# The entry of the two FFNs of a hybrid encoder step: wider vector instructions, another order of operand preparation, and two lent weight tiles

## The chip, the cores and the metric

One core of one Trainium2 chip runs the whole program. The metric is the device time in microseconds of one execution, the median of some runs. TensorE (PE) multiplies matrices; VectorE (DVE), ScalarE (ACT) and GpSimd (POOL) work element by element; SyncE (SP) issues most transfers (DMA). Each engine works through its own instructions in order and waits on semaphores for the others.

## The reference

A two-layer encoder step on 1088 columns (1024 prompt frames and 64 sample frames) of width 1024, all in fp32. Each layer has a mixer (SSD in layer 0, attention in layer 1) and then the SwiGLU FFN, each between two norms:

```
x = x + rmsnorm(mixer(rmsnorm(x, n0)), n1)
x = x + rmsnorm(swiglu(rmsnorm(x, n2), w_in, w_out), n3)
swiglu(u) = (silu(u @ w_gate) * (u @ w_up)) @ w_out
```

The hidden width is 2816, that is 22 slices of 128. The change touches the way from the mixer's projection to the first slices of `swiglu` in both layers, and the weight loads of the rest of the FFN.

## The kernel before, in words

fp32 products are built from reduced-precision ones: every operand is split in a high part (a cast on ACT, "cast") and a low part (operand minus high part, a subtraction on DVE, "low"), and three matmuls h·xh, h·xl, l·xh take the place of one. So each weight tile and each activation tile needs a cast and a low before PE can use it; the first matmul of a product needs both high parts, the second the activation's low, the third the weight's low.

PE's order is written by hand: a planner (`Stream`) spawns side tasks after given delays in modelled PE time (`CHW` holds such delays for the norms). The order on the other engines comes from a scheduler with priorities: code under `tc.high_priority(k)` is issued ahead of lower ones. Once issued the order on an engine is fixed.

The FFN of a layer (`back`) runs so. The columns are in four quarters `QS` of 256, 256, 288 and 288. `start` projects a quarter (`mmx` matmuls); `chain` then applies the post-norm (L1178), adds x (L1179, which arrives by DMA in `xr`, L1169 and L1175), squares (ACT, L449 and L452), sums the squares over eight tiles (POOL, L453), lets PE add over partitions (`nst`, L461), forms the reciprocal root, spreads it (`nbp` on PE, `rb` on ACT, L492) and applies the pre-norm (L1190). Quarters 0 and 1 make block 0 (n = 256 per half), quarters 2 and 3 block 1 (n = 288).

`op_build` makes a block's operands for Strassen-like products: a11, a12, a21, a22 (two halves of the channels by two quarters) and the sums s3, s2, s1, s4 (L1107, L1140). Each is split (cast L1119, low L1120).

First `plain_pairs` runs five slices of block 0 by ordinary products (`mmx`, L427 to L429) on a11 to a22 alone. Then `run_pair` runs double pairs: seven products P1 (weight r0, operand a11), P6 (ta, s2), P2 (r0, a12), P7 (ta, s3), P5 (tb, s1), P4 (tb, a22), P3 (b22, s4) per block, twelve matmuls each, into `px` tiles in PSUM (four of them), whose results DVE and ACT take out (L1257 to L1277). Here r0, b22 are weights, ta and tb sums of them (L262, L263 on POOL, L280, L281 on DVE). In the first double pair, t = 5, block 0's seven products run ahead of block 1's seven (`apart`); afterwards the blocks alternate. At the end stand five single-block pairs and then the product with `w_out` (`po`).

Weights go through a raw ring of two tiles (L224, 512 KB each), then cast L312 and low L313 into a ring `hl` of three. A raw tile is free when its last reader is done, an `hl` slot when PE has read it.

Of the kernel before, what the change touches and what calls it, by code (L numbers as in the profile page):

```python
# [1 line left out]

# [10 lines left out]
ALU = mybir.AluOpType  # L13
# [25 lines left out]

GAP_A, GAP_B = 1.8, 1.2  # L40
RB_WAIT = 4.8
CHW = ((13.1, 8.8, 18.0), (7.5, 6.0, 20.5)), ((9.0, 5.2, 18.0), (10.5, 8.0, 21.0))
AT_W1, AT_W2 = 6.0, 2.5
SSD_GAP, SSD_D = 4.4, 6.5
ST_W, ST_RB = (6.5, 22.0, 22.0), (6.0, 1.0, 1.0)
# [152 lines left out]
            c["ring"][1] += 1  # L198


class Weights:


# [2 lines left out]
    def __init__(self, nc, raw, hl, half, tt):  # L206
        self.nc, self.raw, self.hl, self.half, self.tt = nc, raw, hl, half, tt

        self.tc, self.pri = None, 0
        self.lq, self.sq, self.ready, self.eng = [], [], [], None  # L210

        self.hx, self.used = Ring(None, "hx", 0, hl.shape, hl.dtype), []

    def plan(self, *items):
        for it in items:
            it = dict(it)
            it["raw"] = []
            self.lq.append(it)
            self.sq.append(it)

    def load(self):
        it = self.lq[0]
        r = self.raw.get()
        self.nc.sync.dma_start(r[:, :it.get("n", 1024)], it["src"][len(it["raw"])])  # L224
        it["raw"].append(r)
        if len(it["raw"]) == len(it["src"]):
            self.lq.pop(0)

    def advance(self):
        moved = True  # L230
        while moved:
            moved = False
            while self.lq and self.raw.free():
# [8 lines left out]
    def plain(self, it):  # L242
        if not self.room():
            return False
        r, n = it["raw"][0], it.get("n", 1024)
        if it.get("kscale") is not None:
            self.scaled(it, r)
        else:
            self.part(it, "w", None, r[:, :n])
        self.raw.put()  # L250
        self.ready.append(self.sq.pop(0))
        return True

    def pair(self, it):
        r0, r1 = it["raw"]
        b11, b21, b12, b22 = r0[:, :512], r0[:, 512:], r1[:, :512], r1[:, 512:]
        if "T" not in it:
            if not self.tt.free(2):
                return False
            ta, tb = it["T"] = self.tt.get(), self.tt.get()  # L260
            g = self.nc.gpsimd.tensor_tensor
            g(ta[:, 512:], b22, b12, op=ALU.subtract)  # L262
            g(tb[:, :512], b12, b11, op=ALU.subtract)  # L263
            return True
        ta, tb = it["T"]
        if "b22" not in it and self.half.free():
            self.part(it, "b22", self.half, b22, self.nc.gpsimd)
            self.raw.put()
            return True
        if "r0" not in it:  # L270
            if not self.hl.free():
                return False
            self.part(it, "r0", self.hl, r0)
            self.ready.append(it)

            return False
        if "sums" not in it:
            v = self.nc.vector.tensor_tensor
            with self.tc.high_priority(self.pri):
                v(ta[:, :512], ta[:, 512:], b11, op=ALU.add)  # L280
                v(tb[:, 512:], b21, ta[:, :512], op=ALU.subtract)  # L281
            self.raw.put()
# [64 lines left out]
def hybrid_kernel(  # L347
# [48 lines left out]
    W.tc = tc  # L396
    UC = Cells(384, (R, 99))
    DG = Ring(nsb, "dg", DGB, [P, 3, P])

# [687 lines left out]
    def op_build(ops, done, when=lambda: True):  # L1087
# [14 lines left out]
        def total(nm_, x_, y_, op, eng):  # L1102
            yield 0, 0, R.free if nm_ == "s3" else some
            t, rg[nm_] = take(R) if nm_ == "s3" else take(*rings)
            L[nm_] = v4(t, n)
            with tc.high_priority(OPP[ops.layer][ops.b]):
                eng.tensor_tensor(L[nm_], L[x_], L[y_], op=op)  # L1107
            yield 0, OS[ops.b]

# [22 lines left out]
            ("s1", "a21", "a22", ALU.add, V), ("s4", "a12", "s2", ALU.subtract, V),  # L1132
        )
        if ops.b:
            for x in sums:
                if x[0] not in L:
                    yield from total(*x)
                else:
                    with tc.high_priority(OPP[ops.layer][ops.b]):
# [12 lines left out]
        rg["a12"].put()  # L1152
        for nm_ in ("a21", "a22", "s2", "s1", "s4", "s3"):
            yield from split(nm_)

    def chain(layer, q, y, ss, cw, xsrc, xout, cpre, done):
# [1 line left out]
        o, n = QS[q]  # L1158

        rings = (RX, R) if q < 2 else (R,)  # L1160

        def some():
            return any(r.free() for r in rings)

        w_post, w_rb, w_pre = CHW[layer][q // 2]
        yield 0, w_post, some
        t, r = take(*rings)
        xr = v4(t, n)
        nc.sync.dma_start(xr, xsrc[:, 0:4, o:o + n])  # L1169
        out = []  # L1170
        yield from rb_steps(ss, n, out, w_rb)
        s2 = ssum_start(n)
        for m in range(KD):
            if m == 4:
                nc.sync.dma_start(xr, xsrc[:, 4:8, o:o + n])  # L1175
            ym = y[m // 4][:, m % 4, :]
            with tc.high_priority(CHP[layer][q // 2]):
                V.scalar_tensor_tensor(ym, ym, col(cw + m), out[0], op0=ALU.mult, op1=ALU.mult)  # L1178
                (V if m % 2 else G).tensor_tensor(ym, ym, xr[:, m % 4, :], op=ALU.add)  # L1179
                add_sq(s2, ym, n, m == 0)  # L1180
            if m % 4 == 3:
# [104 lines left out]
    def back(layer, start, cpost, xsrc, xmid, cpre, cpost2, xout, rb_out, done2):  # L1286
# [3 lines left out]
        with ExitStack() as es:  # L1290
# [103 lines left out]
            with ExitStack() as e2:  # L1394
# [27 lines left out]
            phase[0] = 2  # L1422

            W.pri = LDP
            xss, more = {}, None
# [538 lines left out]
```

## Time and profile before

| | us |
|---|---|
| median of 3 runs | 3045.68 (3041.55 to 3046.09) |
| the profiled execution | 3046.85 |
| its span in the trace | 3045.2 |
| PE busy | 2981.5 |
| DVE busy | 2075.4 |
| ACT busy | 1463.6 |
| POOL busy | 816.2 |

Mean granted clock of PE: 0.993. The times of the rows below count from the start of the span. A row of waits says which instruction of an engine waited, for whose result, how long in all and how often. A row of a timeline shows one instruction or a run of like ones; instructions that follow each other directly overlap by some 0.08 us, so the starts tell the spacing. In a row of windows the clock 1.00 is 2.4 GHz and 0.50 is 1.2 GHz.

### The profile page before, as it was taken

To read this page: it belongs to the slowest core of one execution; us is meant where nothing else is said; L and a number is where in the kernel's file an instruction comes from. 1 tells how busy PE (TensorE), PEld (TensorE's weight loads), DVE (VectorE), ACT (ScalarE), POOL (GpSimd) and SP (SyncE) were. 2 spreads that over 40 slices of the span, in tenths; PEclk is the share of its full clock that TensorE was granted. 3 is DMA by queue.
4 is the path that set the end of the run, shared out by engine and by line. 5 is a ranking of instruction groups with operands and counts; after the bars stand their busy time and mean duration, and the time that the engine had idled before them with its cause. 6 is when DMAs were issued, how large, how long until landed. Compare 5 with 4: busy or idle time off the path is not lost. (4 is left out here: it accounts for less than half of the span.)

```text
span 3045.2 us, 56936 instructions
## 1 busy us (share of the span) xinstructions
PE 2981.5 (98%) x21785; PEld 2913.9 (96%) x21785; DVE 2075.4 (68%) x4498; ACT 1463.6 (48%) x2703; POOL 816.2 (27%) x975
## 2 busy tenths in 40 slices
PE   8999999999999999999999999999999999999999
PEld 7899999999999999999999899999999999999998
DVE  7878877786778545584656787777677645575544
ACT  6656666564453222244445665556553322344433
POOL 1323333330434334351222000000154434342111
PEclk9999999999999999999999999999999999999999
DMA  3011111125554222245655222223455222245654
GB/s 120 33 57 51 58 49 50 60 69 154 170 156 129 81 79 77 80 138 177 205 179 158 86 85 72 63 65 100 129 154 154 75 82 78 73 124 179 205 187 139
DMA packets 180097, 333.35 MB, mean 109 GB/s; under 512 B 18128, under 2 KB 128336, under 8 KB 179824
## 3 DMA queue, kind: packets, MB, share of 16 engines
q1 hardware_dynamic: 178032, 323.35, 34.5%
q0 software_dynamic: 1792, 6.36, 1.1%
q8 instruction: 171, 2.80, 0.4%
q14 instruction: 102, 0.84, 0.1%
HBM read 262.59 MB, written 62.60 MB: 107 GB/s over the span
## 5 line engine op out<-in xcount | busy, mean ns | idle before, releaser
L427 PE MATMUL mm<-r,hl 128*128 128x384 f32 (+2 forms) x1664 | 554.7, 333 | 8.4 <-DVE craw L713 4.5
L429 PE MATMUL mm<-r,hl 128*128 128x384 f32 (+2 forms) x1664 | 539.3, 324 | 1.1 <-DVE hl L313 0.6
L428 PE MATMUL mm<-r,hl 128*128 128x384 f32 (+2 forms) x1664 | 538.8, 324 | 0.0
L313 DVE TENSOR_TENSOR hl<-raw,hl 128x1024 fp32r<-128x1024 f32 (+1 forms) x269 | 332.0, 1235 | 299.7 <-ACT hl L312 298.6
L312 ACT CAST hl<-raw 128x1024 fp32r<-128x1024 f32 (+1 forms) x269 | 270.7, 1010 | 263.8 <-DMA raw<-in_w_f_dram 98.8
L1246 PE MATMUL px<-r,hl 128*128 128x288 f32 (+1 forms) x1192 | 349.9, 294 | 0.0
L427 PEld LDWEIGHTS mm<-r,hl 128*128 128x128 f32 x1664 | 315.5, 190 | 11.5 <-issue 5.1
L1245 PE MATMUL px<-r,hl 128*128 128x288 f32 x1056 | 311.5, 295 | 6.1 <-DVE u L1260 6.1
L429 PEld LDWEIGHTS mm<-r,hl 128*128 128x128 f32 x1664 | 314.9, 189 | 2.1 <-DVE hl L325 1.1
L453 POOL TENSOR_TENSOR ssum<-ssum,sq 128x256 f32<-128x256 f32 (+3 forms) x153 | 166.2, 1093 | 559.4 <-ACT sq L452 556.2
L428 PEld LDWEIGHTS mm<-r,hl 128*128 128x128 f32 x1664 | 315.7, 190 | 0.5 <-issue 0.2
L1247 PE MATMUL px<-r,hl 128*128 128x288 f32 x1056 | 310.7, 294 | 0.0
L1247 PE MATMUL px<-rx,hl 128*128 128x256 f32 x816 | 229.3, 281 | 6.7 <-DVE hl L313 6.7
L1245 PE MATMUL px<-rx,hl 128*128 128x256 f32 x816 | 229.8, 282 | 0.0
L1246 PEld LDWEIGHTS px<-r,hl 128*128 128x128 f32 x1192 | 223.9, 188 | 0.1
L1442 PE MATMUL po<-rx,hl 128*128 128x384 f32 (+1 forms) x640 | 206.9, 323 | 0.0
L1245 PEld LDWEIGHTS px<-r,hl 128*128 128x128 f32 x1056 | 198.4, 188 | 8.0 <-DVE u L1260 8.0
L1441 PE MATMUL po<-rx,hl 128*128 128x384 f32 (+1 forms) x608 | 198.5, 326 | 0.0
L1247 PEld LDWEIGHTS px<-r,hl 128*128 128x128 f32 x1056 | 198.2, 188 | 0.0
L1443 PE MATMUL po<-rx,hl 128*128 128x384 f32 (+1 forms) x608 | 197.0, 324 | 0.4 <-DVE hl L313 0.3
L1246 PE MATMUL px<-rx,hl 128*128 128x256 f32 x680 | 190.8, 281 | 0.0
L262 POOL TENSOR_TENSOR tt<-raw 128x512 f32<-128x512 f32 x44 | 60.0, 1364 | 402.7 <-DMA raw<-in_w_f_dram 274.5
(359 smaller groups left out, 8141.5 us busy)
## 6 DMA issues: line engine op xcount, KB each, us to landing
raw<-in_w_f_dram SPq DMA_DIRECT2D x204, 512.0 KB, 3.8
raw<-in_w_in_dram SPq DMA_DIRECT2D x40, 512.0 KB, 3.7
raw<-in_w_f_dram SPq DMA_DIRECT2D x48, 384.0 KB, 3.2
sg<-hscr SPq DMA_DIRECT2D x88, 192.0 KB, 3.6
raw<-in_w_so_dram SPq DMA_DIRECT2D x32, 512.0 KB, 3.9
raw<-in_w_kv_dram SPq DMA_DIRECT2D x18, 512.0 KB, 3.6
raw<-in_w_o_dram SPq DMA_DIRECT2D x16, 512.0 KB, 3.7
sg<-hscr SPq DMA_DIRECT2D x44, 160.0 KB, 3.7
```

The costliest lines, as they stand in the source:

```text
L312: self.nc.scalar.copy(h, v)
L313: (eng or self.eng or self.nc.vector).tensor_tensor(lo, v, h, op=ALU.subtract)
L427: PE.matmul(ps[:, :n], h_, xh, start=(first and i == 0), stop=False)
L428: PE.matmul(ps[:, :n], h_, xl, start=False, stop=False)
L429: PE.matmul(ps[:, :n], l_, xh, start=False, stop=(last and i == nk - 1))
L453: (eng or G).tensor_tensor(ssum[:, :n], ssum[:, :n], q[:, :n], op=ALU.add)
L1245: PE.matmul(ps, wh, ah[:, k, :], start=(k == 0), stop=False)
L1246: PE.matmul(ps, wh, al[:, k, :], start=False, stop=False)
L1247: PE.matmul(ps, wl, ah[:, k, :], start=False, stop=(k == 3))
L1441: PE.matmul(ps[:, :n], wh, xh, start=(k == 0), stop=False)
L1442: PE.matmul(ps[:, :n], wh, xl, start=False, stop=False)
L1443: PE.matmul(ps[:, :n], wl, xh, start=False, stop=(k == FT - 1))
```

## The change

Four parts. (1) `chain` takes two `xr` tiles and loads all of x's quarter at its start; the add and the square run on four tiles at once (add on DVE alone), and the sum of the squares is three DVE additions of 1024, 512 and 256 columns; POOL is no longer in it. In layer 1 the second norm of quarters 0 and 1 is planned after 13 instead of 18 us. (2) `op_build` of block 0 splits a11, a12, a21, a22 ahead of all sums. (3) `op_build` of block 1 waits for `W.lead`, the low part of `ta` of the first double pair, and its sums are issued after it. (4) From the last double pair on, up to two operand tiles `RX` serve as further raw weight tiles, one in the `w_out` stage, none at its very end.

```diff
+class Lent:
+    def __init__(self, ring):
+        self.ring, self.cap, self.live = ring, 0, 0
+    def free(self):
+        return self.live < self.cap and self.ring.free()
...
-CHW = ((13.1, 8.8, 18.0), (7.5, 6.0, 20.5)), ((9.0, 5.2, 18.0), (10.5, 8.0, 21.0))
+CHW = ((13.1, 8.8, 18.0), (7.5, 6.0, 20.5)), ((9.0, 5.2, 13.0), (10.5, 8.0, 21.0))
...
+        if key == "ta" and self.lead is None:
+            self.lead = ins
...
-            with tc.high_priority(OPP[ops.layer][ops.b]):
+            with tc.high_priority(OPP[ops.layer][ops.b]), (tc.issue_after(W.lead.ins) if ops.b else nullcontext()):
                 eng.tensor_tensor(L[nm_], L[x_], L[y_], op=op)
...
         if ops.b:
+            yield 0, 0, lambda: W.lead is not None
             for x in sums:
...
-        for nm_ in ("a11", "a12"):
+        for nm_ in ("a11", "a12", "a21", "a22"):
             yield from split(nm_, True)
         for x in sums:
             yield from total(*x)
...
-        for nm_ in ("a21", "a22", "s2", "s1", "s4", "s3"):
+        for nm_ in ("s2", "s1", "s4", "s3"):
             yield from split(nm_)
...
-        for m in range(KD):
-            if m == 4:
-                nc.sync.dma_start(xr, xsrc[:, 4:8, o:o + n])
-            ym = y[m // 4][:, m % 4, :]
-            with tc.high_priority(CHP[layer][q // 2]):
-                V.scalar_tensor_tensor(ym, ym, col(cw + m), out[0], op0=ALU.mult, op1=ALU.mult)
-                (V if m % 2 else G).tensor_tensor(ym, ym, xr[:, m % 4, :], op=ALU.add)
-                add_sq(s2, ym, n, m == 0)
...
+        with tc.high_priority(CHP[layer][q // 2]):
+            for h in range(2):
+                for m in range(4):
+                    ym = y[h][:, m, :]
+                    V.scalar_tensor_tensor(ym, ym, col(cw + 4 * h + m), out[0], op0=ALU.mult, op1=ALU.mult)
+                V.tensor_tensor(y[h], y[h], xr[h], op=ALU.add)
+                A.activation(xr[h], y[h], AF.Square)
+                nc.sync.dma_start(xout[:, 4 * h:4 * h + 4, o:o + n], y[h])
+            V.tensor_tensor(xr[0], xr[0], xr[1], op=ALU.add)
+            V.tensor_tensor(xr[0][:, 0:2, :], xr[0][:, 0:2, :], xr[0][:, 2:4, :], op=ALU.add)
+            V.tensor_tensor(s2[:, :n], xr[0][:, 0, :], xr[0][:, 1, :], op=ALU.add)
...
                     if t_ == FT - 1:
                         phase[0] = 1
+                        W.lent.cap = 2
                         st.spawn(loader())
```

What this does to the order on DVE, at three places. First, layer 1, where block 0's operands are made. Before, L1190 is the pre-norm of quarter 1, L1107 the sums, L1120 the lows (the row 3040 is that of a21):

```order
3035 L1120 TENSOR_TENSOR rx<-rx 128x1024 x2
3036 L1190 SCALAR_TENSOR_TENSOR rx<-rx,pcs,rb 128x256 x8
3037 L1107 TENSOR_TENSOR r<-rx 128x1024
3038 L1107 TENSOR_TENSOR rx<-rx,r 128x1024
3039 L1107 TENSOR_TENSOR rx<-rx 128x1024 x2
3040 L1120 TENSOR_TENSOR r<-rx,r 128x1024
3041 L1120 TENSOR_TENSOR rx<-rx 128x1024
```

In the changed kernel the same lines are L1218 (pre-norm), L1132 (sums) and L1145 (lows):

```order
3050 L1145 TENSOR_TENSOR rx<-rx 128x1024
3051 L1218 SCALAR_TENSOR_TENSOR rx<-rx,pcs,rb 128x256 x8
3052 L1145 TENSOR_TENSOR rx<-rx 128x1024
3053 L1145 TENSOR_TENSOR r<-rx,r 128x1024
3054 L1145 TENSOR_TENSOR rx<-rx 128x1024
3055 L1132 TENSOR_TENSOR r<-rx 128x1024
3056 L1132 TENSOR_TENSOR rx<-rx,r 128x1024
3057 L1132 TENSOR_TENSOR rx<-rx 128x1024 x2
```

All four lows of a11 to a22 now stand ahead of the sums.

Second, layer 0, the first double pair. Before, L1107 and L1140 are block 1's sums, the first two L313 the lows of ta and tb, L1260 to L1266 take products of block 0 out of PSUM, and the first L1120 is the low of block 1's a11:

```order
1269 L1107 TENSOR_TENSOR r<-r 128x1152 x2
1270 L1140 TENSOR_TENSOR r<-r 128x1152
1271 L313 TENSOR_TENSOR hl<-tt,hl 128x1024
1272 L1221 TENSOR_TENSOR x<-mmx,x 128x256
1273 L1107 TENSOR_TENSOR r<-r 128x1152
1274 L313 TENSOR_TENSOR hl<-tt,hl 128x1024
1275 L1260 TENSOR_TENSOR u_11425<-px,p_11410 128x256
1276 L280 TENSOR_TENSOR tt<-tt,raw 128x512
1277 L1120 TENSOR_TENSOR r<-r 128x1152
1278 L1262 TENSOR_TENSOR p_11410<-px,p_11410 128x256
1279 L1266 TENSOR_TENSOR u_11463<-px,u_11425 128x256
1280 L281 TENSOR_TENSOR tt<-raw,tt 128x512
```

In the changed kernel L335 is the low of ta and then of tb, L302 and L303 are weight sums of the next pair, L1132 and L1167 block 1's sums, L1288 to L1300 the evictions of block 0's products:

```order
1285 L335 TENSOR_TENSOR hl<-tt,hl 128x1024
1286 L1132 TENSOR_TENSOR r<-r 128x1152
1287 L1249 TENSOR_TENSOR x<-mmx,x 128x256
1288 L335 TENSOR_TENSOR hl<-tt,hl 128x1024
1289 L302 TENSOR_TENSOR tt<-tt,raw 128x512
1290 L1288 TENSOR_TENSOR u_11330<-px,p_11315 128x256
1291 L303 TENSOR_TENSOR tt<-raw,tt 128x512
1292 L1132 TENSOR_TENSOR r<-r 128x1152
1293 L1290 TENSOR_TENSOR p_11315<-px,p_11315 128x256
1294 L1167 TENSOR_TENSOR r<-r 128x1152
1295 L1294 TENSOR_TENSOR u_11363<-px,u_11330 128x256
1296 L1132 TENSOR_TENSOR r<-r 128x1152
```

and, right behind these, the evictions of P5 and P4 and the low of block 1's a11 (L1145):

```order
1297 L1297 TENSOR_TENSOR c_11378<-px,u_11363 128x256
1298 L1298 TENSOR_TENSOR u_11330<-px,u_11330 128x256
1299 L1300 TENSOR_TENSOR u_11363<-px,u_11363 128x256
1300 L1145 TENSOR_TENSOR r<-r 128x1152
```

The sums moved from ahead of the low of ta to behind it, in between the evictions; the low of a11 moved behind the eviction of P4, the sixth of block 0's seven products.

Third, the end of the same pair, block 1's products. Before, the last of the seven lows (L1120) is that of s4; the three L313 are the lows of r0, ta and tb of the next pair:

```order
1289 L1120 TENSOR_TENSOR r<-r 128x1152
1290 L1262 TENSOR_TENSOR p_11535<-px,p_11535 128x288
1291 L1120 TENSOR_TENSOR r<-r 128x1152
1292 L313 TENSOR_TENSOR hl<-raw,hl 128x1024
1293 L1266 TENSOR_TENSOR u_11591<-px,u_11554 128x288
1294 L313 TENSOR_TENSOR hl<-tt,hl 128x1024
1295 L1269 TENSOR_TENSOR c_11613<-px,u_11591 128x288
1296 L1270 TENSOR_TENSOR u_11554<-px,u_11554 128x288
1297 L1272 TENSOR_TENSOR u_11591<-px,u_11591 128x288
1298 L313 TENSOR_TENSOR hl<-tt,hl 128x1024
1299 L1277 TENSOR_TENSOR u_11554<-px,u_11554 128x288
```

In the changed kernel the three L335 are these lows, L1300 is the eviction of block 1's P4, and the last L1145 is the low of s4:

```order
1307 L335 TENSOR_TENSOR hl<-raw,hl 128x1024
1308 L1294 TENSOR_TENSOR u_11495<-px,u_11454 128x288
1309 L335 TENSOR_TENSOR hl<-tt,hl 128x1024
1310 L1297 TENSOR_TENSOR c_11521<-px,u_11495 128x288
1311 L1298 TENSOR_TENSOR u_11454<-px,u_11454 128x288
1312 L1300 TENSOR_TENSOR u_11495<-px,u_11495 128x288
1313 L335 TENSOR_TENSOR hl<-tt,hl 128x1024
1314 L1145 TENSOR_TENSOR r<-r 128x1152
```

The low of s4 moved from ahead of all three weight lows to behind them and behind the eviction of P4. Layer 1's first pair has the same order at its end, rows 3157 to 3164.

## Rows read from the trace of the kernel before

**Rows 1.** The page: busy time by engine, and one of its groups.

```profile
PE 2981.5 (98%) x21785; PEld 2913.9 (96%) x21785; DVE 2075.4 (68%) x4498; ACT 1463.6 (48%) x2703; POOL 816.2 (27%) x975
...
L1245 PE MATMUL px<-r,hl 128*128 128x288 f32 x1056 | 311.5, 295 | 6.1 <-DVE u L1260 6.1
```

**Rows 2.** Waits of PE, 2240 to 2372 us: us in total, times, longest.

```profile
PE px L1247 <- DVE hl L313: 3.0, 1, 3.0
PE mmx L428 <- DVE r L1120: 2.5, 1, 2.5
PE mmx L427 <- ACT hl L312: 1.8, 1, 1.8
PE mmx L429 <- DVE hl L313: 0.8, 1, 0.8
```

**Rows 3.** Timeline of PE: start, us, operation, in brackets the idle time ahead and releaser.

```profile
961.54 0.58 PE L1247 MATMUL px<-rx,hl 128*128 128x256 f32 x1 [3.71 <-DVE hl L313]
...
2257.03 0.83 PE L461 MATMUL nst<-ones,ssum 128*128 128x1 f32 x4 [3.59 <-POOL ssum L453]
```

**Rows 4.** Windows: us, busy of PE, PEld, DVE, ACT, POOL, clock, DMA, GB/s.

```profile
972.28:983.45 11.17, 11.17 (x86) 11.17 (x85) 11.17 (x13) 7.26 (x9) 3.08 (x2) 1.00 0.11 30
2281.18:2287.97 6.79, 6.79 (x32) 6.79 (x33) 5.82 (x16) 3.46 (x5) 0.02 (x1) 0.50 1.05 249
2322.11:2328.93 6.82, 6.82 (x34) 6.82 (x33) 4.29 (x15) 0.00 (x0) 0.00 (x0) 0.50 0.66 216
2345.22:2371.28 26.06, 22.94 (x170) 22.44 (x169) 25.15 (x28) 13.73 (x17) 8.82 (x5) 0.93 0.25 79
2349.94:2352.83 2.89, 2.89 (x13) 2.89 (x14) 2.89 (x3) 2.89 (x5) 2.41 (x2) 0.50 0.14 45
```

**Rows 5.** Timeline of DVE, first pair of layer 0: start, us, line, operation.

```profile
967.97 1.35 DVE L1120 TENSOR_TENSOR r<-r 128x1152 fp32r<-128x1152 f32 x1
...
969.57 0.41 DVE L1266 TENSOR_TENSOR u<-px,u 128x256 f32<-128x256 f32 x1
969.90 0.67 DVE L281 TENSOR_TENSOR tt<-raw,tt 128x512 f32<-128x512 f32 x1
...
974.37 3.37 DVE L1120 TENSOR_TENSOR r<-r 128x1152 fp32r<-128x1152 f32 x2
```

**Rows 6.** Timeline of ACT, same stretch; in brackets idle before, and releaser.

```profile
960.34 0.62 ACT L312 CAST half<-raw 128x512 fp32r<-128x512 f32 x1 [5.53 <-DMA raw<-in_w_f_dram]
960.86 1.04 ACT L312 CAST hl<-tt 128x1024 fp32r<-128x1024 f32 x1
```

**Rows 7.** Timeline of POOL, same stretch.

```profile
962.61 2.42 POOL L262 TENSOR_TENSOR tt<-raw 128x512 f32<-128x512 f32 x1
966.19 1.30 POOL L263 TENSOR_TENSOR tt<-raw 128x512 f32<-128x512 f32 x1 [1.16 <-DVE hl L313]
...
974.79 1.73 POOL L1278 TENSOR_TENSOR c<-p,u 128x256 f32<-128x256 f32 x1
```

**Rows 8.** Timeline of DVE, layer 1, quarters 0 and 1.

```profile
2228.79 2.63 DVE L1178 SCALAR_TENSOR_TENSOR rx<-rx,pcs,rb 128x256 f32<-128x256 f32 x4
...
2270.17 3.81 DVE L1190 SCALAR_TENSOR_TENSOR rx<-rx,pcs,rb 128x256 f32<-128x256 f32 x8 [2.32 <-ACT rb L492]
```

**Rows 9.** Timeline of ACT, layer 1, before the first pair.

```profile
2318.01 0.44 ACT L452 ACTIVATE sq<-r 128x288 f32<-128x288 f32 x1 [0.44 <-POOL ssum L453]
...
2318.62 1.98 ACT L312 CAST hl<-raw 128x1024 fp32r<-128x1024 f32 x2
...
2333.72 1.06 ACT L312 CAST hl<-raw 128x1024 fp32r<-128x1024 f32 x1 [1.48 <-PE mmx L429]
...
2338.62 0.62 ACT L312 CAST half<-raw 128x512 fp32r<-128x512 f32 x1 [1.26 <-DMA raw<-in_w_f_dram]
```

**Rows 10.** Timeline of DVE, first pair of layer 1.

```profile
2368.33 1.34 DVE L1120 TENSOR_TENSOR r<-r 128x1152 fp32r<-128x1152 f32 x1
...
2373.33 1.21 DVE L313 TENSOR_TENSOR hl<-tt,hl 128x1024 fp32r<-128x1024 f32 x1
```

More of the change, by code (lines that the diff above doesn't have):

```diff
@@ L1 @@
-from contextlib import ExitStack
+from contextlib import ExitStack, nullcontext
 import concourse.bass as bass
@@ L198, in put, with get @@
             c["ring"][1] += 1
+class Lent:
[3 more added lines that the diff above has]
+        return self.live < self.cap and self.ring.free()
+    def get(self):
+        self.live += 1
+        return self.ring.get()
+    def put(self):
+        self.live -= 1
+        self.ring.put()
 class Weights:
@@ L210, in __init__ @@
         self.lq, self.sq, self.ready, self.eng = [], [], [], None
+        self.raws, self.lent, self.lead = [raw], None, None
         self.hx, self.used = Ring(None, "hx", 0, hl.shape, hl.dtype), []
@@ L216, in plan @@
             it = dict(it)
-            it["raw"] = []
+            it["raw"], it["of"] = [], []
             self.lq.append(it)
@@ L222, in load @@
         it = self.lq[0]
-        r = self.raw.get()
+        ring = next(r for r in self.raws if r.free())
+        r = ring.get()
+        it["of"].append(ring)
         self.nc.sync.dma_start(r[:, :it.get("n", 1024)], it["src"][len(it["raw"])])
@@ L232, in advance @@
             moved = False
-            while self.lq and self.raw.free():
+            while self.lq and any(r.free() for r in self.raws):
                 self.load()
@@ L249, in plain @@
             self.part(it, "w", None, r[:, :n])
-        self.raw.put()
+        it["of"][0].put()
         self.ready.append(self.sq.pop(0))
@@ L267, in pair @@
             self.part(it, "b22", self.half, b22, self.nc.gpsimd)
-            self.raw.put()
+            it["of"][1].put()
             return True
@@ L281, in pair @@
                 v(tb[:, 512:], b21, ta[:, :512], op=ALU.subtract)
-            self.raw.put()
+            it["of"][0].put()
             it["sums"] = True
@@ L395, in hybrid_kernel @@
     )
-    W.tc = tc
+    W.tc, W.lent = tc, Lent(RX)
+    W.raws.append(W.lent)
     UC = Cells(384, (R, 99))
@@ L1138, in op_build @@
                 else:
-                    with tc.high_priority(OPP[ops.layer][ops.b]):
+                    with tc.high_priority(OPP[ops.layer][ops.b]), tc.issue_after(W.lead.ins):
                         x[4].tensor_tensor(L[x[0]], L[x[1]], L[x[2]], op=x[3])
@@ L1151, in op_build @@
                 rg["a11"].put()
-        rg["a12"].put()
-        for nm_ in ("a21", "a22", "s2", "s1", "s4", "s3"):
+        for nm_ in ("a12", "a21", "a22"):
+            rg[nm_].put()
+        for nm_ in ("s2", "s1", "s4", "s3"):
             yield from split(nm_)
@@ L1160, in chain @@
         rings = (RX, R) if q < 2 else (R,)
-        def some():
-            return any(r.free() for r in rings)
         w_post, w_rb, w_pre = CHW[layer][q // 2]
[L1166 to L1169, printed above, removed]
+        yield 0, w_post, lambda: sum(r.bufs - r.live for r in rings) >= 2
+        got = [take(*rings) for _ in range(2)]
+        xr = [v4(t, n) for t, _ in got]
+        for h in range(2):
+            nc.sync.dma_start(xr[h], xsrc[:, 4 * h:4 * h + 4, o:o + n])
         out = []
@@ L1399, in back @@
                 ops[0].yring, ops[1].yring = RX, R
+                W.lead = None
                 start(ops, px, lambda q, y, ss: st.spawn(chain(layer, q, y, ss, cpost, xsrc, xmid, cpre, dn)), dn)
@@ L1419, in back @@
                         phase[0] = 1
+                        W.lent.cap = 2
                         st.spawn(loader())
                 W.tt.bufs = W.half.bufs = 0
-            phase[0] = 2
+            phase[0], W.lent.cap = 2, 1
             W.pri = LDP
@@ L1431, in back @@
                 for m in range(KD):
+                    if s == NSL - 1 and m == KD - 1:
+                        W.lent.cap = 0
                     ps = px.tile([P, 512], F32, tag="mm", name="po")
```

8 lines of the change are left out of this document (4 added, 4 removed).

## The prediction

> **What bounds the kernel now.** I read the page first: PE is busy 98% of the span, DVE 68% [rows 1]. So an edit to DVE, ACT or POOL is worth only what it takes from PE's idle time. Then the waits of PE, entry by entry: in layer 1 four waits of 0.8 to 3.0 us, on the low of a21, on a weight cast and its low, and on the low of ta in the first pair [rows 2], and one of 3.6 on POOL's sum of squares; in layer 0 one of 3.7 on the low of ta [rows 3]. Last the windows: after such a wait PE runs at 0.50, the 1.2 GHz level, for 2.9 to 6.8 us, even after the 1.8 us wait for the weight cast [rows 4]. Half of that is lost: 3.4 after the low of a21, 3.4 after the weight cast, 1.5 after the low of ta. For other waits I take 1.5 and keep 3.4 as the upper end. So one new wait of 3 us costs some 5.
>
> **The wide chain (part 1).** In layer 1 quarter 1's sum released PE at 2257.0, 3.6 us late [rows 3]. The new chains of quarters 0 and 1 on DVE, from 2228.8 [rows 8]: 16 multiplies, at 0.47 (eight in 3.81) or 0.64 (four in 2.63), are 7.5 to 10.2 us; four wide adds and two wide sums, of the size of a 1024-column low (1.21, [rows 10], less the overlap of 0.08), 6.8; the short sums, bounded by the 512-column operation (0.67) and an eviction (0.33 between starts, [rows 5]), 1.9; two weight lows between them 2.3; small ones about 0.5. That is 19.0 to 21.7, so the sum ends at 2247.8 to 2250.5. PE's request for it moves too: quarter 1's sum over partitions stands 48 matmuls of 288 columns earlier, 0.13 each by block 1's 86 in 11.17 us [rows 4], so PE comes at 2253.4 less 6.2, 2247.2. A wait of 0.6 to 3.3 remains, near 2. From 3.6 plus a drop of 1.5 I take a gain of 3.0, between 1.5 and 5.1. The second half of x is now loaded ahead of weight loads on SP; I price that at zero since the weight casts there wait for PE to free slots (the cast at 2333.72, [rows 9]).
>
> The wide squares also end the weight wait: the cast at 2318.62 stood behind a square that waited for POOL [rows 9]. With POOL out of the chain it goes early: 1.8, 0.8 and 3.4 us, gain 6.0, at least 2.6 if a short wait and the drop stay.
>
> **Lows before sums (part 2).** The low of a21 was 2.5 us late and stood behind four sums of 1.2 each, 4.8. It now stands ahead of them, with 2.3 to spare. Gain 2.5 and 3.4, together 5.9. The sums are needed only in the first pair, at 2345 [rows 4], so being later costs nothing. Sum of layer 1's gains: 14.9, between 10 and 17.
>
> **Block 1 behind the lead (part 3): layer 0's first pair.** The low of ta no longer waits behind three sums (L1107, L1140), so its 3.7 goes. But the low of tb needs the cast at 960.86, which stands behind the half's cast, held by a transfer till 960.34 [rows 6]. That stays: the low of tb ends near 963.1. Then the new order on DVE: L302 waits for POOL, whose sum ends at 965.0 [rows 7], and ends at 965.7; an eviction 0.33; L303 behind POOL's other sum (1.30), till 967.0; then three sums (1.27 between starts, as the low of 1152 columns, [rows 5]), five evictions (0.33) and the low of a11 (1.35): 6.8. Block 1 starts near 973.8 instead of 972.3, the end of the seven products before. Its products take 11.2 [rows 4]. Inside them the second new wait: P3's second matmul needs the low of s4, which stands behind the low of the next tb. That one's cast needs the slot that PE frees at the end of block 1's P4. So from the end of P4: a cast 1.04, a low 1.22, the low of s4 1.34 [rows 6, 10], 3.6 us, with PE idle. Before, the low of s4 was done 5 us ahead of the low of tb [rows 10]. Both waits bring a drop, 1.5 each. End: 973.8 + 11.2 + 3.6 + 3.0 = 991.6 against 983.5. Loss 8.1; at least 5 (start 972.5, one drop), at most 13 (974.5, two drops of 3.4).
>
> **Layer 1's first pair.** Its two blocks took 26.1 us [rows 4]; less 11.2 for block 1's products, block 1 started 14.9 after block 0. In the new order the low of ta stands behind most of the pre-norm and its cast behind the next half's, so I leave its 3.0 as it is. From there DVE has tb's low, L302, L303, four sums, seven evictions and the low of a11, some 12 us by the durations above: block 1 starts at 14.5 to 18, I take 16.5. With the products, the 3.6 of s4 and 3.0 for drops it ends at 34.3. Loss 8.2, between 5 and 11.
>
> **Lent tiles (part 4).** The single pairs' waits are all on an eviction (6.1 us in the whole program, [rows 1]), not on a weight. Earlier raw tiles can help only through DVE's order: I take 1 us, between 0 and 6.
>
> **Sum.** −14.9 + 8.1 + 8.2 − 1 = +0.4 on the profiled 3046.85, so 3047.3. The median of the runs shown is 1.2 lower, so the forecast is 3046.1: no change that can be told, where 0.2% (6 us) is about what a measurement of this kernel can tell.
>
> **The rivals.** *Faster A: only the low of s4 is late.* If DVE reaches block 1's a11 when it does now, each pair loses only 3.6 and 1.5: −14.9 + 10.2 − 1 = −5.7, 3040. For it: my 12 us and 6.8 us take no slack from lows and sums that may run while the chain waits for POOL. Against: the low stands behind six evictions, which wait for PE. *Faster B: neither wait comes.* If the next tb's cast finds its slot free before P4 ends, the low of s4 comes in time; only the gains are left, and layer 0 adds its 3.7 and a drop of 1.5: −14.9 − 5.2 − 1 = −21, 3025. Against: PE's last use of this tb frees that slot, now as before, and the low of the next tb came 5 us after that of s4 [rows 10].
>
> *Slower C: the first pair of layer 1 is set by the weights, not by PE.* The half's cast at 2338.62 waited for its transfer [rows 9]. If PE arrives 12 us earlier and the transfer doesn't, the two later gains (11.9) come back as a wait for ta: 3046.1 + 11.9 = 3058. For it: that transfer. Against: its raw tile was freed after a cast that waited for PE (2333.72, [rows 9]), so it moves with PE. It decides once more than 6 of the 11.9 come back.
>
> *Slower D: POOL slows DVE in the pairs.* Two lows of block 1 took 3.37 instead of 2.62 beside POOL's L1278 [rows 5, 7]. If all such work lies under DVE's path, each pair pays about 2.3 more (three POOL operations at 0.75): 3050.7. The Trainium skill (GPSIMD Engine Reference, section Specifications) says that POOL shares its SBUF interfaces with VectorE and contends with VectorE instructions that have two SBUF inputs. By that rule every sum and low of block 1, which now lies later, beside L1274 and L1278, would be slowed, and the wide chain, freed of POOL, would be as short as my lower end; the trace agrees for the lows with 3.37 against 2.62. These two sides nearly cancel, 4.6 lost and 2.7 won.
>
> *The change doesn't do what it says:* for the lent tiles this is in the sum at 1 us; for the rest the order shows it done.
>
> **How the numbers follow.** Likeliest, both waits and the layer-1 gains: 0.48, own range 3039 to 3053. A 0.18, B 0.08, C 0.16, D 0.10. Of the likeliest, 0.34 lie within 0.2% (3039.6 to 3051.8), 0.06 below and 0.08 above; A is split, D mostly inside. So faster 0.26, same 0.48, slower 0.26. The range reaches down past A and up to C: 3035 to 3058, leaving out B and what of C lies beyond.
>
> **What would show it.** Right: in both first pairs PE waits for a low of the line L1145 ahead of block 1, and again for one of some 3.6 us in its last product; the waits on POOL's sum, on the low of a21 and on the weight cast are gone or short; the entry of layer 1 ends some 10 us earlier at the first pair's start. Wrong: the pair of layer 0 ends near 983 (A or B), or the first pair of layer 1 waits over 6 us for ta (C). Then the time is off by the amount named there.

## The result and the profile after

Over 11 runs each the changed kernel has a median of 3048.05 us (3042.84 to 3056.30), the kernel before 3043.55 (3039.61 to 3046.09). The ratio is 1.0019, 95% interval 1.0010 to 1.0027: slower beyond its interval, by less than the 0.2% that the forecast allowed for "no change". The forecast was 3046.1 with a range of 3035 to 3058. The profiled execution took 3050.39 us, its span is 3048.7.

The page after, busy time, against [rows 1]:

```profile
PE 2982.2 (98%) x21785; PEld 2918.2 (96%) x21785; DVE 2058.6 (68%) x4506; ACT 1456.7 (48%) x2655; POOL 741.4 (24%) x887
```

PE does the same work, POOL 75 us less. Where the time went shows in the waits. Waits of PE after, layer 0, 950 to 1000 us (columns as in [rows 2]), against the one wait of [rows 3]:

```profile
PE px L1274 <- DVE r L1145: 6.3, 2, 4.2
PE px L1273 <- DVE u L1288: 1.9, 1, 1.9
PE px L1275 <- DVE hl L335: 0.8, 1, 0.8
PE px L1273 <- DVE p L1290: 0.5, 1, 0.5
```

and layer 1, 2230 to 2380 us, against [rows 2, 3]:

```profile
PE px L1274 <- DVE r L1145: 9.2, 2, 5.0
PE nst L486 <- DVE ssum L1209: 2.6, 1, 2.6
PE px L1273 <- ACT hl L334: 2.0, 1, 2.0
PE px L1275 <- DVE hl L335: 0.8, 1, 0.8
PE px L1273 <- DVE u L1288: 0.4, 1, 0.4
```

L1145 is the line of the operands' lows, L1209 the end of the wide chain, L334 and L335 are weight casts and lows, L1288 and L1290 evictions. The waits on the low of a21, on POOL's sum and on the weight cast ahead of the first pair are gone, though PE still waits 2.6 us for the wide chain's own sum; in their place both pairs wait twice on L1145. Timeline of all engines after, end of layer 0's pair:

```profile
986.65 1.04 ACT L334 CAST hl<-tt 128x1024 fp32r<-128x1024 f32 x1 [1.09 <-PE px L1275]
...
987.73 1.23 DVE L335 TENSOR_TENSOR hl<-tt,hl 128x1024 fp32r<-128x1024 f32 x1 [0.26 <-ACT hl L334]
988.12 1.48 POOL L1302 TENSOR_TENSOR u<-u,c 128x288 f32<-128x288 f32 x1 [10.45 <-ACT u L1301]
...
988.87 1.95 DVE L1145 TENSOR_TENSOR r<-r 128x1152 fp32r<-128x1152 f32 x1
989.57 2.41 POOL L284 TENSOR_TENSOR tt<-raw 128x512 f32<-128x512 f32 x1
...
990.87 0.61 PE L1274 MATMUL px<-r,half 128*128 128x288 f32 x1 [4.18 <-DVE r L1145]
```

This is the second new wait, read from the last row upwards: P3 waits 4.18 us for the low of s4 at 988.87, which stood behind the weight low at 987.73, which waited for its cast at 986.65, which waited for PE's end of P4. The forecast had 1.04 + 1.22 + 1.34 = 3.6; the low of s4 took 1.95 beside POOL's L1302 and L284. Timeline of DVE after, layer 1, in front of block 1:

```profile
2357.53 1.34 DVE L1132 TENSOR_TENSOR r<-r 128x1152 f32<-128x1152 f32 x1
2358.80 0.41 DVE L1305 TENSOR_TENSOR u<-px,u 128x256 f32<-128x256 f32 x1
2359.13 5.88 DVE L1145 TENSOR_TENSOR r<-r 128x1152 fp32r<-128x1152 f32 x4
```

The last sum, the eviction of P3 and only then the low of a11 (first of the four at 2359.13): PE waited 5.0 us for it. Windows after (columns as in [rows 4]): block 1 in layer 0 and in layer 1, then the stretches of half clock that follow their waits:

```profile
972.90:993.70 20.80, 14.48 (x87) 14.02 (x86) 19.12 (x22) 9.90 (x12) 8.18 (x5) 0.83 0.14 46
2355.30:2379.70 24.40, 15.20 (x87) 14.74 (x86) 21.59 (x24) 10.96 (x13) 8.15 (x5) 0.78 0.12 39
976.20:979.60 3.40, 3.40 (x17) 3.40 (x16) 3.17 (x3) 1.97 (x3) 1.47 (x1) 0.50 0.23 77
990.87:996.70 5.83, 5.83 (x25) 5.83 (x26) 2.84 (x3) 0.79 (x2) 4.04 (x4) 0.50 0.01 4
2360.73:2365.50 4.77, 4.77 (x20) 4.77 (x21) 4.29 (x3) 2.20 (x4) 0.53 (x1) 0.50 0.09 28
2376.87:2382.50 5.63, 5.63 (x25) 5.63 (x26) 2.83 (x3) 0.62 (x1) 3.84 (x4) 0.50 0.01 3
```

Block 1 takes 20.8 and 24.4 us for products that took 11.17 before in layer 0 [rows 4]. Each stretch at 0.50, the 1.2 GHz level, follows one of the waits and costs half its length (the "drop" of the prediction): 1.7 and 2.9 us in layer 0, 2.4 and 2.8 in layer 1.

Lengths of the stages in us, each the difference between the starts of two matmuls in PE's timeline (entry: first `mmx` of layer 1 to the first product of its first pair; pair: first product of the first pair to that of the second; singles: first single pair to the first `po`). The ratio is to the kernel before as measured beside that run; its median was 3043.57 beside e1 to e4, 3042.73 beside e5 to e8 and 3038.39 beside e9 and e10, so runs of different groups are compared by their ratios:

| kernel | entry 1 | pair, layer 0 | pair, layer 1 | singles 0 / 1 | ratio to before |
|---|---|---|---|---|---|
| before | 169.6 | 27.4 | 26.1 | 59.5 / 60.4 | |
| changed | 156.7 | 35.8 | 38.1 | 55.8 / 55.8 | 1.0019 (1.0010 to 1.0027) |
| e1 no lead | 156.7 | 25.7 | 38.5 | 55.8 / 55.8 | 0.9983 (0.9974 to 0.9993) |
| e2 s4 first | 156.7 | 30.8 | 33.0 | 55.8 / 56.0 | 0.9975 (0.9964 to 0.9986) |
| e3 part 4 alone | 164.4 | 27.3 | 25.9 | 56.2 / 56.1 | 0.9977 (0.9966 to 0.9988) |
| e4 part 2 alone | 166.9 | 27.4 | 38.2 | 58.9 / 58.4 | 1.0036 (1.0023 to 1.0048) |
| e5 e1 and e2 | 156.7 | 25.8 | 32.3 | 56.0 / 55.8 | 0.9973 (0.9962 to 0.9984) |
| e6 block 1 first | 156.7 | 35.3 | 37.9 | 55.8 / 56.1 | 1.0018 (1.0009 to 1.0027) |
| e7 part 1 alone | 155.3 | 25.7 | 36.9 | 59.4 / 58.3 | 0.9999 (0.9989 to 1.0010) |
| e8 order of need | 156.7 | 32.1 | 33.8 | 55.8 / 56.0 | 0.9989 (0.9980 to 0.9998) |
| e9 e5, norm at 16 | 158.3 | 25.8 | 28.5 | 55.8 / 56.1 | 0.9955 (0.9941 to 0.9968) |
| e10 parts 1 and 4, norm at 16 | 156.7 | 25.9 | 26.9 | 56.3 / 56.0 | 0.9959 (0.9947 to 0.9972) |
| e11 before again | 168.3 | 26.4 | 26.9 | 59.8 / 59.5 | |
| e12 changed again | 156.7 | 35.6 | 38.1 | 55.9 / 56.1 | |

### The profile page after: what moved, and what is told of

It is laid out like the page before. It is cut to its first block, busy times and chain, and to the rows that moved or that the text cites. A ratio compares the mean times of both kernels' runs of the same rounds, so it can differ in the third digit from the quotient of the medians.

```text
span 3048.7 us, 56713 instructions
## 1 busy us (share of the span) xinstructions
PE 2982.2 (98%) x21785; PEld 2918.2 (96%) x21785; DVE 2058.6 (68%) x4506; ACT 1456.7 (48%) x2655; POOL 741.4 (24%) x887
## 5 line engine op out<-in xcount | busy, mean ns | idle before, releaser
L335 DVE TENSOR_TENSOR hl<-raw,hl 128x1024 fp32r<-128x1024 f32 (+1 forms) x215 | 274.4, 1278 | 237.2 <-ACT hl L334 235.4
L334 ACT CAST hl<-raw 128x1024 fp32r<-128x1024 f32 (+1 forms) x215 | 223.8, 1046 | 247.0 <-PE po L1475 166.3
L478 POOL TENSOR_TENSOR ssum<-ssum,sq 128x256 f32<-128x256 f32 (+3 forms) x97 | 121.4, 1253 | 564.6 <-ACT sq L477 551.4
L1274 PEld LDWEIGHTS px<-r,hl 128*128 128x128 f32 x1192 | 225.9, 189 | 7.6 <-DVE r L1145 7.6
L1273 PEld LDWEIGHTS px<-r,hl 128*128 128x128 f32 x1056 | 200.6, 190 | 0.0
L1275 PEld LDWEIGHTS px<-r,hl 128*128 128x128 f32 x1056 | 200.3, 190 | 0.0
L284 POOL TENSOR_TENSOR tt<-raw 128x512 f32<-128x512 f32 x42 | 59.3, 1411 | 429.9 <-DMA raw<-in_w_f_dram 282.6
```

The source lines that it names most:

```text
L335: ins = (eng or self.eng or self.nc.vector).tensor_tensor(lo, v, h, op=ALU.subtract)
L478: (eng or G).tensor_tensor(ssum[:, :n], ssum[:, :n], q[:, :n], op=ALU.add)
L1273: PE.matmul(ps, wh, ah[:, k, :], start=(k == 0), stop=False)
L1274: PE.matmul(ps, wh, al[:, k, :], start=False, stop=False)
L1275: PE.matmul(ps, wl, ah[:, k, :], start=False, stop=(k == 3))
```

## The experiments

The theory: the order on DVE in the two first pairs costs what the entry of layer 1 and the single pairs gain. The rivals: one part alone is to blame in both layers; contention or the lent tiles cost the time; DVE has too much to do in the pair, whatever the order.

**e1, the changed kernel without part 3.**

```diff
-            with tc.high_priority(...), (tc.issue_after(W.lead.ins) if ops.b else nullcontext()):
+            with tc.high_priority(...):
...
-            yield 0, 0, lambda: W.lead is not None
...
-                    with tc.high_priority(...), tc.issue_after(W.lead.ins):
+                    with tc.high_priority(...):
```

> The changed kernel without its part 3 (block 1 does not wait for the lead, its sums are not issued after it). In DVE's order that moves only layer 0: three sums stand ahead of the low of ta again and the low of s4 ahead of the low of the next tb; layer 1's order stays as in the changed kernel. Theory (order): layer 0's first pair gets its 3.7 us wait on ta back and loses the waits of 2.1 and 4.2 on L1145 and their drops: block 1 takes 11 to 12 us instead of 20.8, the pair 27 to 29 instead of 35.8; layer 1's two waits of 5.0 and 4.2 stay. Median about 8 us below the changed kernel, 3040. Rival (contention or lent tiles cost the time, not the order): both pairs stay slow, median 3047 to 3049. Rival (part 3 alone is to blame, in both layers): layer 1's pair also falls back to 26 us, median 3028.

Median 3038.48. Waits of PE, layer 0's pair, then layer 1's:

```profile
PE px L1274 <- DVE hl L335: 2.9, 1, 2.9
```

```profile
PE px L1273 <- DVE r L1145: 8.8, 2, 4.6
```

Layer 0's two waits are gone and 2.9 us on the low of ta are back; layer 1 keeps both of its waits (8.8 us). So part 3 makes layer 0's loss, and not layer 1's.

**e2, s4's cast and low above the weights.**

```diff
-            with tc.high_priority(OPP[ops.layer][ops.b]):
+            with tc.high_priority(3500 if ops.b and nm_ == 's4' else OPP[ops.layer][ops.b]):
                 A.copy(h, L[nm_])
```

> The changed kernel with one priority raised: the cast and low of block 1's s4 go ahead of the weights' lows. Theory (order): the wait of 4.2 us in the last product of block 1 goes in both layers, with most of its drop (up to 3.4): block 1 takes 13 to 15 us in layer 0 (20.8 in the changed kernel) and 16 to 18 in layer 1 (24.3); the waits of 2.1 and 5.0 ahead of block 1 stay. Median 13 to 15 us below the changed kernel, 3033 to 3035, under the kernel before. Rival (the low of the next tb is now late instead): PE waits 1 to 4 us for it in the next pair, gain under 8 us, 3040 to 3045. Rival (not the order): no change, 3048.

Median 3036.45, a little above the expected 3033 to 3035. Block 1 took 15.6 us in layer 0 and 18.4 in layer 1, and the only wait on L1145 left in layer 1 was that for a11:

```profile
PE px L1274 <- DVE r L1145: 4.3, 1, 4.3
```

No wait for the next tb took its place: that rival fell.

**e3, part 4 alone.** Against the kernel before:

```diff
+    W.raws.append(W.lent)
...
+                        W.lent.cap = 2
...
-            phase[0] = 2
+            phase[0], W.lent.cap = 2, 1
```

> The kernel before with part 4 alone (lent raw tiles). Theory: entries and first pairs as in the kernel before (169.6 us to layer 1's first pair, 26.1 us in it); the single pairs take 55.8 us in both layers instead of 59.5 and 60.4; in layer 0's last stage the wait of 2.7 us on a weight's low and its drop are there (271.8 instead of 269.4 us). Median 3043.6 less 8.3 plus 1 to 2.4, 3036 to 3038. Rival (the single pairs got faster through the other parts): 59 to 60 us there, median 3043 to 3046.

Median 3034.59, below the expected 3036 to 3038. The single pairs wait for nothing and take 56.2 and 56.1 us; the last stage of layer 0 has its 2.7 us wait on a weight's low. So the lent tiles alone make that gain. The entry was 164.4, not 169.6, with the same order of instructions (see e11).

**e4, part 2 alone.** Against the kernel before:

```diff
-        for nm_ in ("a11", "a12"):
+        for nm_ in ("a11", "a12", "a21", "a22"):
             yield from split(nm_, True)
...
-        for nm_ in ("a21", "a22", "s2", "s1", "s4", "s3"):
+        for nm_ in ("s2", "s1", "s4", "s3"):
```

> The kernel before with part 2 alone (block 0's four lows ahead of its sums). In PE's order layer 1's norms of quarters 2 and 3 stand 49 matmuls later than before and on DVE the sums of block 1 stand behind the low of ta, the low of s4 behind the next tb's. Theory (order, and part 2 is what makes it so in layer 1): layer 1's entry loses the 2.5 us wait on a21 (about 6 us shorter with its drop, 163 to 164), its first pair has waits of some 5 and 4 us on L1120 and takes 36 to 39 us instead of 26.1; layer 0 is as before. Median 3048 to 3051. Rival (part 1 or part 3 makes layer 1's order): the first pair stays at 26 to 28 us, median 3037 to 3040.

Median 3054.68, the slowest of all and above the expected 3048 to 3051. Waits of PE in layer 1:

```profile
PE px L1247 <- DVE r L1120: 9.2, 2, 5.0
PE mmx L429 <- DVE hl L313: 3.8, 1, 3.8
```

L1120 is here the line of the lows. Part 2 alone makes both waits in layer 1's pair (38.2 us). The wait on a21 is gone, but one of 3.8 us on a weight's low came into the entry, which shrank only to 166.9.

**e5, e1 and e2 together.** Against e1:

```diff
-            with tc.high_priority(OPP[ops.layer][ops.b]):
+            with tc.high_priority(3500 if ops.b and nm_ == 's4' else OPP[ops.layer][ops.b]):
```

> The changed kernel without part 3 and with the low of block 1's s4 ahead of the weights' lows: the two edits of the first two runs together. Theory (order; layer 0's loss is part 3's, layer 1's is part 2's and stands on s4 and a11): layer 0's first pair as without the lead (25.7 us to its end), layer 1's as with s4 first (33.0), entries as in the changed kernel (156.7). Sum from the stages: 3036.5 less 5.1, or 3038.5 less 7.0, both 3031 to 3032; about 12 us under the kernel before. Rival (the two gains are one and the same): 3036 to 3038.

Median 3034.37: both gains hold at once (25.8 and 32.3 us), the total 2 to 3 us above the expected 3031 to 3032.

**e6, block 1 above all.** The sums, casts and lows of block 1 at priority 3500, without part 3.

```diff
-            with tc.high_priority(OPP[ops.layer][ops.b]):
+            with tc.high_priority(3500 if ops.b else OPP[ops.layer][ops.b]):
...
```

> The changed kernel without part 3, and all casts, sums and lows of block 1 above weights and evictions. On DVE block 1's sums and six lows stand in one run ahead of the evictions of block 0's second product and later ones. Theory (what PE waits for at block 1's start is the low of a11): the wait of 4.3 to 5 us on L1145 in layer 1 goes, its pair takes 27 to 30 us; median 3026 to 3030. Rival (DVE's work in the pair is the bound, whatever the order: 11 operations of 1.27 us, four PSUM tiles): PE waits 4 us or more for evictions (u and p lines) instead, in both layers; layer 0's pair 29 to 33 us, layer 1's 31 to 36; median 3031 to 3038.

Median 3048.60. The theory for this run fell. Timeline of all engines, layer 1's pair:

```profile
2356.02 7.69 DVE L1145 TENSOR_TENSOR r<-r 128x1152 fp32r<-128x1152 f32 x6
...
2363.63 0.41 DVE L1289 TENSOR_TENSOR p<-px,p 128x256 f32<-128x256 f32 x1
...
2364.09 0.58 PE L1272 MATMUL px<-rx,half 128*128 128x256 f32 x1 [10.10 <-DVE p L1289]
```

Six lows run without a break (7.69 us), and only then comes the eviction of P2 (L1289): PE stood still for 10.1 us, its next product waiting for that tile. In layer 0 it waited 8.5 us for weights' lows. So the waits moved, as the rival has it, but the rival's own numbers (pairs of 29 to 36 us, 3031 to 3038) were too low as well. DVE's work alone doesn't set these pairs. Windows of layer 1's pair (columns as in [rows 4]) in e6, in the changed kernel and in e10 below:

```profile
2340.41:2378.36 37.95, 23.62 (x170) 22.82 (x169) 30.02 (x40) 15.84 (x20) 5.98 (x6) 0.87 0.16 50
2341.53:2379.67 38.14, 25.86 (x170) 24.67 (x169) 33.43 (x41) 15.49 (x20) 12.47 (x8) 0.86 0.17 54
2324.71:2351.62 26.91, 22.80 (x171) 22.60 (x169) 26.88 (x28) 13.72 (x17) 7.09 (x5) 0.94 0.19 62
```

In e10, as in the kernel before (25.15 of 26.06 us [rows 4]), DVE is busy nearly all the time, so there the pair can get no shorter than this work. In e6 and in the changed kernel more of that work falls into the pair (30.0 and 33.4 us), and DVE is idle for 7.9 and 4.7 us besides: both the late start of the work and its order cost time.

**e7, part 1 alone.** Against the kernel before, besides the chain's new body:

```diff
-CHW = (...), ((9.0, 5.2, 18.0), (10.5, 8.0, 21.0))
+CHW = (...), ((9.0, 5.2, 13.0), (10.5, 8.0, 21.0))
...
-                (V if m % 2 else G).tensor_tensor(ym, ym, xr[:, m % 4, :], op=ALU.add)
-                add_sq(s2, ym, n, m == 0)
+                V.tensor_tensor(y[h], y[h], xr[h], op=ALU.add)
+                A.activation(xr[h], y[h], AF.Square)
```

> The kernel before with part 1 alone (wide chain, earlier second norm). In PE's order layer 1's norms of quarters 2 and 3 stand some 36 matmuls later than before, and on DVE the low of s4 stands behind the next tb's in layer 1 again. Theory: POOL's sum is no longer what PE waits for, but a wait of some 2.6 us stays on the wide chain's own sum, since PE asks 6 us earlier; the weight-cast wait goes; the a21 wait stays; layer 1's entry 160 to 164 us instead of 169.6. Its first pair 34 to 38 us. Layer 0 as before. Median 3044 to 3050. Rival (only part 2 disturbs the first pair of layer 1): pair at 26 to 28, median 3035 to 3038. Rival (the wide operations gain nothing): entry 168 to 170.

Median 3041.32, below the expected 3044 to 3050; the entry is below the expected 160 to 164. Waits of PE, layer 1:

```profile
PE px L1246 <- DVE r L1120: 5.4, 2, 4.0
PE px L1245 <- ACT hl L312: 4.4, 1, 4.4
PE nst L461 <- DVE ssum L1181: 2.6, 1, 2.6
```

The entry is as short as with all parts (155.3), and the wait on a21, which was expected to stay, is gone without part 2. Part 1 also holds the second norm planned after 13 instead of 18 us; what the wide operations and this delay each give was not tried apart. But part 1 too makes layer 1's pair long (36.9).

**e8, block 1 in the order of need.** The cast and low of a11 ahead of all sums, s4 last, all at 3500, without part 3. Against e6:

```diff
-            for x in sums:
...
+            yield from split("a11", True)
+            yield from total(*by["s3"])
...
+            yield from total(*by["s2"])
+            yield from split("s2", True)
+            yield from split("a12", True)
+            yield from split("s3")
...
+            yield from total(*by["s4"])
...
+            yield from split("s4")
```

> As the run with block 1 above all, but with block 1's operands made in the order in which PE needs them: low of a11 before any sum, then s3, s2, their lows and a12's, s1, a22, last s4. Theory (a11's low comes early, the rest just in time): layer 1's pair 26 to 30 us, layer 0's 24 to 27; median 3025 to 3030. Rival (DVE's work in the pair is the bound): the waits move to later lows or to evictions, layer 1's pair 31 to 36; median 3031 to 3036.

Median 3039.41, above both expectations; pairs of 32.1 and 33.8 us, with a wait of 6.7 us on a weight's low in layer 0 and of 4.1 on an eviction in layer 1. The rival again: what comes early for block 1 comes at the cost of block 0.

**e9, e5 with an earlier norm.** What is left is to give DVE the work sooner.

```diff
-CHW = (...), ((9.0, 5.2, 13.0), (10.5, 8.0, 21.0))
+CHW = (...), ((9.0, 5.2, 13.0), (10.5, 8.0, 16.0))
```

> The fifth run's kernel (no part 3, s4 first) with layer 1's second norm of quarters 2 and 3 planned after 16 instead of 21 us. On DVE block 1's first two sums then stand ahead of the low of ta again. Theory (layer 1's pair waits for a11 because its norms come late): the wait of 5.0 us on L1145 there goes, with its drop; a wait of 1 to 3 us on ta takes its place; the pair takes 25 to 29 us instead of 32.3; median 4 to 7 us below the fifth run, 3027 to 3030. Rival (the norm is asked for too early): PE waits 2 to 5 us for the sum of squares of quarters 2 and 3 and the entry grows from 156.7 to 159 to 162; no gain. Rival (a11 waits for something else): pair stays at 31 to 33.

Median 3026.12, by its ratio some 5 us under e5, though the two intervals overlap a little. Waits of PE, layer 1:

```profile
PE px L1274 <- DVE hl L335: 3.3, 1, 3.3
PE nst L486 <- DVE ssum L1208: 2.6, 1, 2.6
PE px L1273 <- DVE r L1145: 0.5, 1, 0.5
```

The last line is no wait for a11. Timeline of all engines, block 1's last product:

```profile
2357.68 1.35 DVE L1145 TENSOR_TENSOR r<-r 128x1152 fp32r<-128x1152 f32 x1
...
2359.08 0.40 PE L1273 MATMUL px<-r,half 128*128 128x288 f32 x1 [0.54 <-DVE r L1145]
```

It is P3 (weight b22, a `half` tile) waiting for s4. The 5.0 us for a11 are gone, the low of ta takes 3.3 again, and the pair takes 28.5. So layer 1's wait for a11 came from the late norms of quarters 2 and 3. The entry took 158.3: the stretch of half clock behind the wait of 2.6 us lasted 6.8 us here and 3.4 in e5.

**e10, parts 1 and 4 with the earlier norm.** Against the changed kernel, besides the norm's 16.0: `op_build` as in the kernel before.

```diff
-            yield 0, 0, lambda: W.lead is not None
...
-        for nm_ in ("a11", "a12", "a21", "a22"):
+        for nm_ in ("a11", "a12"):
             yield from split(nm_, True)
```

> Parts 1 and 4 alone, with the norm of quarters 2 and 3 after 16 us; operands of both blocks made as in the kernel before. Theory (parts 2 and 3 bring nothing that part 1 doesn't): layer 1's entry 155 to 157 us, its pair 25 to 29, layer 0's pair 25.7, single pairs 55.8; median 3026 to 3031, about 15 us under the kernel before. Rival (part 2 is needed once the rest is faster): the wait on the low of a21 returns, 2.5 us and up to 3.4 of drop, entry 159 to 163; median 3031 to 3036.

Median 3026.46, 0.4% under the kernel before and equal to e9. Waits of PE, layer 1:

```profile
PE px L1272 <- DVE hl L335: 4.1, 1, 4.1
PE nst L486 <- DVE ssum L1206: 2.6, 1, 2.6
```

No wait on a21: parts 2 and 3 are not needed for the gain. Nor is there one on s4, which e7 has (4.0 us) with the norm at 21, though no priority was raised; so in layer 1 that wait too goes with the late norms.

**e11 and e12, both kernels unchanged, a second profile each.** No edit.

> The kernel before once more, unchanged, for a second profile: the run with part 4 alone took 164.4 us for layer 1's entry although its order there is that of the kernel before, which took 169.6. Theory (the stage's length depends on where the stretches of half clock fall in one execution): layer 1's entry comes out between 163 and 170 us, not at 169.6, while the first pairs stay within 0.5 us of 27.4 and 26.1. Rival (part 4 changes the entry in a way that the order doesn't show): 169.6 within 0.5.

> The changed kernel once more, unchanged, for a second profile. Six kernels with its chain had 156.7 us for layer 1's entry. Theory: 156.7 within 0.5 again, layer 0's pair 35.8 and layer 1's 38.1 within 1.5; both waits on L1145 in both pairs. Rival (the waits vary from execution to execution by several us): pair lengths off by more than 2 us.

One run each, 3047.81 and 3048.70. The entry of the kernel before took 168.3, its pairs 26.4 and 26.9, off the expected 27.4 and 26.1 by up to 1.0; the changed kernel repeats its stages within 0.3. So the kernel before has an entry of 164.4 to 169.6, by execution, and the gain there is 8 to 13 us. In the changed kernel the split between the two blocks does not repeat: in e12 the waits for a11 were 3.2 and 3.4 us instead of 2.1 and 5.0, but its low was ready 17.2 and 19.7 us after the pair's first product, against 17.4 and 19.2. DVE sets that moment, whenever PE comes to it.

## Why the prediction was right

The total was right because gains and losses nearly cancel, as forecast: both first pairs lose by two waits each on L1145, at the places named and behind the instructions named. That the total was met to 2 us is also luck: by the two first profiles the four terms below were off by +2.0, +1.7, +4.8 and −6.2, which cancel to +2.3. The sizes of the terms:

- **Layer 1's gains** (−14.9): the entry shrank by 12.9. The waits on a21 and on the weight cast went (5.9 and 6.0). The term for the sum of squares, 3.0, was mis-sized: the wait shrank from 3.6 to 2.6 and the drop stayed, 1.0 in all, outside its 1.5 to 5.1. The forecast had a wait of 0.6 to 3.3 remain and left no drop behind it.
- **Layer 0's pair** (+8.1): 8.4, and 1.4 of the last drop fall in the next pair (the sixteen following pairs take 336.4 instead of 335.0). Here the parts held too: the second matmul of block 1 ran 17.4 us after the pair's first product, the forecast's 973.8 is 17.7 after that of the kernel before. That match holds two errors that cancel: POOL's sum came 7.9 us after the first product and not 8.9, and L302 took 1.77 us and not 0.67 (first line below). The wait for s4 was 4.2 instead of 3.6.
- **Layer 1's pair** (+8.2): 12.0, and 1.0 in the next pairs, outside its 5 to 11. Block 1's a11 was ready 19.2 us after the first product, not 16.5, and the two drops cost 2.4 and 2.8, not 1.5 each. Between the end of the low of ta and that of a11's DVE took 14.3 us, not some 12: two pieces of the pre-norm (L1218) and an addition (L1249) came in between, L302 waited 0.9 us for POOL, and L303 took 1.80 us beside POOL's L285.
- **Lent tiles** (−1, bounded by 6): −3.7 and −4.6 in the single pairs, +2.4 and −1.3 in the last stages, −7.2 in all. This term failed: "Earlier raw tiles can help only through DVE's order: I take 1 us". The waits of 6.1 us were not the whole loss. In which step of DVE's order the gain arises was not tried.

Timeline of DVE and POOL after, layer 0 (first line) and layer 1:

```profile
965.82 1.77 DVE L302 TENSOR_TENSOR tt<-tt,raw 128x512 f32<-128x512 f32 x1 [1.19 <-POOL tt L284]
...
2344.98 1.23 DVE L335 TENSOR_TENSOR hl<-tt,hl 128x1024 fp32r<-128x1024 f32 x1 [1.03 <-ACT hl L334]
2346.12 0.51 DVE L1218 SCALAR_TENSOR_TENSOR r<-r,pcs,rb 128x288 f32<-128x288 f32 x1
2346.55 0.42 DVE L1249 TENSOR_TENSOR x<-mmx,x 128x256 f32<-128x256 f32 x1
2347.84 0.69 DVE L302 TENSOR_TENSOR tt<-tt,raw 128x512 f32<-128x512 f32 x1 [0.87 <-POOL tt L284]
...
2349.74 1.52 POOL L285 TENSOR_TENSOR tt<-raw 128x512 f32<-128x512 f32 x1 [1.94 <-DVE hl L335]
2350.01 1.80 DVE L303 TENSOR_TENSOR tt<-raw,tt 128x512 f32<-128x512 f32 x1
```

Sum: −12.9 + 9.8 + 13.0 − 7.2 = +2.7; the spans differ by 3.5. The rest is +1.8 ahead of layer 0's first pair and −1.0 in layer 1's attention. The first holds layer 0's own chains, which part 1 changes too; but that pair starts between 955.2 and 960.0 us in the profiles with the wide chain and between 955.5 and 959.1 in those without, so no effect can be told there.

Two steps of the argument were wrong though the total hid it. "Lows before sums (part 2)" was given the 5.9 us of a21; e7 and e10 have that gain without part 2, and e4 shows that part 2 by itself makes layer 1's pair 12 us longer. So "being later costs nothing", as the forecast says of the sums there, was wrong. And for layer 1's pair the forecast named no part of its own, behind a paragraph on part 3; e1 shows that without part 3 nothing changes there. What does it is that the second norms of quarters 2 and 3 stand some 36 (part 1) to 48 (part 2) matmuls later in PE's order, so block 1's sums fall behind the low of ta; e9 moves the norm back and the wait for a11 goes. Which tile or delay makes the planner start them later was not tried.

Of the rivals, A and B fell (both waits came), C too: the first product on ta waited 2.0 and 0.8 us, not over 6. D was real, and about as large as allowed. The low of s4 took 1.95 us beside POOL instead of 1.34, and the four lows at 2359.13 took 5.88 instead of 5.16 (four at 1.27 and the overlap): 1.3 us. L303 above, 1.80 instead of 0.67, makes it 2.4 in layer 1's pair against the 2.3 priced. These weight sums were as slow in the kernel before (L280, 1.67 and 1.79 us in the two pairs); the forecast took them at 0.67. The Trainium skill (GPSIMD Engine Reference, section Specifications) names this contention for VectorE instructions with two SBUF inputs; the trace agrees for these operations.

## What to carry to other kernels

On an engine that works in order, a step that waits for another engine's slot (here a weight cast that needs PE's last use) holds back everything behind it: put what is needed first ahead of it, as e2 does, and count the instructions behind a new wait, not the wait alone. Where the engine is nearly full in a stretch, raising a whole block's work only chose who waits (e6, e8); what helped was to let its work arrive earlier (e9). And time the parts of a bundle apart: here two parts (1 and 4, with one delay changed) gave 0.4%; in the bundle the order that part 3 made in layer 0, and the later norms that parts 1 and 2 made in layer 1, took it back.

## What the runs showed beyond that

With the same order of instructions, the entry of layer 1 of the kernel before took 169.6, 168.3 and (in e3) 164.4 us. The stretches of half clock fell differently: three of them (3.4, 6.8 and 6.8 us) in the first, three (6.8, 3.4 and 6.8) in e11, one of 6.8 in e3. The wait on POOL's sum was 3.6 us in all three; behind it the wait on a21 was 2.5, 1.6 and 1.1, that on the weight cast 1.8, 1.5 and 0.7. The shortest stretch behind POOL's sum (3.4 us against 6.8 and 6.8) goes with the longest wait on a21. A PE that runs at 1.2 GHz comes later to its next wait, which would shorten it; that this links the two was not tried by itself. A wait of this kind read from one execution can be off by a factor of two.
